# Sums of activations for the seven block products on VectorE instead of GpSimd, and other pairs of the down projection that take seven products

## The chip, the cores and the metric

The kernel runs on one core of one Trainium2 chip. The metric is the device time of one execution in microseconds (us); smaller is better. The kernel before took 1475.7 us, the median of three runs (1475.5 to 1476.75).

## The reference

One decoder layer for 256 tokens of width 2048, in float32: a normalised input is projected; a gated delta-rule branch and a block-sparse attention branch are mixed by gates and added to the residual; then a SwiGLU feed-forward follows. The change touches the last part alone:

```python
u = _rmsnorm(h, norm_ffn_w[l])
hid = jax.nn.silu(jnp.einsum('btd,df->btf', u, w_ffn_gate[l])) * jnp.einsum('btd,df->btf', u, w_ffn_up[l])
h = h + jnp.einsum('btf,fd->btd', hid, w_ffn_down[l])
```

The feed-forward width (`DFF`) is 5632, so `hid` has 44 slices (`kc`) of 128 features, and the down projection multiplies 256 x 5632 by 5632 x 2048.

## The kernel before, in words

**Split operands.** Every float32 operand is split into a rounded part (`hi`) and a rest (`lo`), and one product is three matmuls: hi·hi (L283), hi·lo (L284), lo·hi (L285). Weights are streamed from memory by SyncE in units of 128 x 1024 (L74, seven buffers). For each unit ScalarE casts the `hi` half (L87, tile `whi`) and VectorE subtracts it (L88, tile `wlo`); both have four buffers, and a unit is split three ahead of its use, so that the cast of a unit waits until TensorE is done with the unit four before it. The queues of ScalarE and VectorE are worked off in order: whatever stands ahead of a cast holds it back.

**Super jobs.** `super_job` works out two blocks of 512 columns for all 256 tokens at a time. Its weights come in pairs of units (`p`, 22 pairs in the down projection). A direct pair takes eight block products (24 matmuls). A pair marked as seven takes seven block products (21 matmuls), by Winograd's scheme: VectorE makes four half-unit sums of weights (L96, L97, L99, L100), four plan items instead of two are split (`b11`, half a unit, `b2`, and two called `t`), and four sums of activations are needed, for which `make_sums` has one call a pair. The feed-forward has eleven jobs with the pairs 3 and 5 as seven; the down projection has two jobs (`DOWN_USED`), the first with five seven pairs, the second with eight.

**`make_sums` (L962).** It adds hi and lo of two slices of activations (L967, 128 x 512, tile `f`), makes four 128 x 128 sums of the quarters (L970 to L973, tile `t`), casts them on ScalarE (L975, to `dsum` or `usum`) and subtracts the cast on VectorE (L976). `f` and `t` take the two buffers of `fsum` in turn, so the next pair's `t` waits for this pair's L975 and L976. Before the change L967 to L973 are on GpSimd. `down_sums` calls it for the eight pairs of `DOWN_PAIRS`; it is advanced by `tick()`, two ticks a pair of weights, after the five of the last feed-forward job's `swiglu`.

**After the last seven pair of a job** `after` copies four banks (L996) and GpSimd adds them up (L997 to L1000, and L1057 in the down projection).

The order of each engine's queue is set by a scheduler from the program, not by the order of the lines alone.

Of the kernel before, what the change touches and what calls it, by code (L numbers as in the profile page):

```python
# [17 lines left out]
T = 256  # L18
# [20 lines left out]

FFN_PAIRS = (3, 5)  # L40
FFN_ORDER = [[0, 1, 2, 4, 6, 3, 5, 7]] + [list(range(KM // 2))] * (DFF // 512 - 1)
DOWN_PAIRS = (4, 8, 12, 15, 18, 2, 6, 10)
DOWN_USED = [(4, 8, 12, 15, 18), DOWN_PAIRS]


def _super_jobs():

    jobs = [[(p, p in FFN_PAIRS) for p in order] for order in FFN_ORDER]
    return jobs + [[(p, p in used) for p in range(KF // 2)] for used in DOWN_USED]

# [62 lines left out]
def layer(ctx: ExitStack, tc: tile.TileContext, xT, xtok, params, consts, relt, w_bd, w, out):  # L113
    nc = tc.nc
# [193 lines left out]
    with tc.tile_pool(name="xin", bufs=4) as xin:  # L308
# [4 lines left out]
        for u in range(1, RAW):  # L313
            W.load(u)
            if u % 2:
                c = u // 2 + 1
# [632 lines left out]
    def hid(kc, n=1):  # L949
        t, k = (low, kc) if kc < H else (later["high"], kc - H)  # L950
        return t[:, k] if n == 1 else t[:, k:k + n]

    def fft(name, bufs):
        return later["ff"].tile([P, 512], F32, name=name, tag=name, bufs=bufs)
# [8 lines left out]
    def make_sums(g, c):  # L963

        c = c.bitcast(F32)
        f = fft("fsum", 2).rearrange("p (k t) -> p k t", k=2)
        nc.gpsimd.tensor_add(f, c[:, :, :T], c[:, :, T:])  # L967
        a11, a21, a12, a22 = f[:, 0, :P], f[:, 0, P:], f[:, 1, :P], f[:, 1, P:]
        t = fft("fsum", 2).rearrange("p (k t) -> p k t", k=4)
        nc.gpsimd.tensor_add(t[:, 0], a21, a22)  # L970
        nc.gpsimd.tensor_sub(t[:, 1], t[:, 0], a11)
        nc.gpsimd.tensor_sub(t[:, 2], a11, a21)
        nc.gpsimd.tensor_sub(t[:, 3], a12, t[:, 1])  # L973
        yield
        nc.scalar.copy(g[:, 0], t)  # L975
        nc.vector.tensor_sub(g[:, 1], t, g[:, 0].bitcast(F32))  # L976
        yield

# [2 lines left out]
    def ffn_setup():  # L981
        by_stage.close()
        later["ff"] = ff = ctx.enter_context(tc.tile_pool(name="ff", bufs=1))
        later["high"] = ff.tile([P, KF - H, 512], F32R, name="high")
        yield
        for p in FFN_PAIRS:
            usums[p] = ff.tile([P, 2, 4, P], F32R, name="usum", tag="sum", bufs=2)
            yield from make_sums(usums[p], uT[:, 2 * p:2 * p + 2])
# [41 lines left out]

    dsum = acts.tile([P, len(DOWN_PAIRS), 2, 4, P], F32R, name="dsum", tag="actA")

    def down_sums():
        for i, p in enumerate(DOWN_PAIRS):
            yield from make_sums(dsum[:, i], hid(2 * p, 2))
# [10 lines left out]
    chains.append(down_sums())  # L1046
    down = {p: lambda i=i: dsum[:, i] for i, p in enumerate(DOWN_PAIRS)}
    for j in range(2):
# [122 lines left out]
```

## Time and profile before

| | us |
|---|---|
| median of three runs | 1475.7 |
| the profiled execution | 1475.54 |
| its span, first to last instruction | 1473.8 |
| TensorE busy in the span | 1458.2 |
| VectorE busy | 1078.7 |
| ScalarE busy | 759.9 |
| GpSimd busy | 200.9 |

The profiled execution has 1.7 us around its span and lies 0.16 us under the median. Times in the rows below are us from the span's start. TensorE's matmuls are pipelined: each lasts about 0.39 us and a new one starts every 0.23 us, so a busy share near 1 says only that there was no gap. "Idle before" in brackets is the time in which the engine had nothing running before that row, with what ended it. The granted clock of TensorE is 1.00 at 2.4 GHz and 0.50 at 1.2 GHz.

### The profile page before, as it was taken

The page shows a single profiled execution, that of the slowest core. Times are in us where ns is not written, and L with a number is a line of the kernel's source. Part 1 is how long each engine was busy: PE and PEld are TensorE (multiplying, and loading weights), DVE is VectorE, ACT ScalarE, POOL GpSimd, SP SyncE. Part 2 cuts the span into 40 slices and gives each one's busy share as a digit, 9 for nine tenths or more (in the row PEclk, how much of TensorE's full clock was granted, in tenths as well). Part 3 has the DMA queues.
Part 4 walks back from the last instruction along what each step waited for, and adds up shares of the span by engine and source line. Part 5 has one row for each costly group of instructions (what it writes and reads, how often), then busy time and mean ns, then how long its engine had stood idle before and what let it go on. Part 6 is the DMA issues. An engine that isn't in the chain of part 4 may idle for free.

```text
span 1473.8 us, 19231 instructions
## 1 busy us (share of the span) xinstructions
PE 1458.2 (99%) x7077; PEld 1213.5 (82%) x7077; DVE 1078.7 (73%) x1452; ACT 759.9 (52%) x1100; POOL 200.9 (14%) x148
## 2 busy tenths in 40 slices
PE   9999999999999999999999999999999999899998
PEld 8888788888888888888888888888888887688887
DVE  6887679777664455555569888888888887777885
ACT  6664446635454444444545555555555554444553
POOL 0011000020000000000021223022222116405003
PEclk9999999999999999999999999999999999899999
DMA  9457545575456666668756666565665556557763
GB/s 375 147 197 183 162 136 176 163 170 186 143 159 180 195 195 186 189 191 258 217 173 200 214 191 193 170 203 187 214 207 192 190 184 198 163 197 224 231 204 109
DMA packets 78735, 282.05 MB, mean 191 GB/s; under 512 B 8880, under 2 KB 9520, under 8 KB 78256
## 3 DMA queue, kind: packets, MB, share of 16 engines
q1 hardware_dynamic: 76032, 272.30, 59.3%
q0 software_dynamic: 1472, 5.24, 1.1%
q10 hardware_dynamic: 1136, 3.28, 1.0%
q8 instruction: 55, 0.90, 0.2%
q14 instruction: 40, 0.33, 0.1%
HBM read 276.46 MB, written 4.33 MB: 191 GB/s over the span
## 4 chain that ended last, share of the span: by engine, by line
PE 93%; DVE 3%; ACT 1%; issue 1%; POOL 1%; DMA 0%; SPq 0%; DVEq 0%; POOLq 0%; ACTq 0%
PE ps L283 13%; PE ps L284 13%; PE ps L285 13%; PE ps L218 11%; PE ps L219 11%; PE ps L220 11%; PE ps L199 6%; PE ps L200 3%; PE pw L284 2%; PE pw L285 2%; PE pw L283 2%; PE pT L299 1%; DVE wlo L88 1%; ACT whi L87 1%; DVE dsum L976 0%
## 5 line engine op out<-in xcount | busy, mean ns | idle before, releaser
L88 DVE TENSOR_TENSOR wlo<-wraw,whi 128x1024 fp32r<-128x1024 f32 (+1 forms) x575 | 702.8, 1236 | 282.1 <-ACT whi L87 277.0
L87 ACT CAST whi<-wraw 128x1024 fp32r<-128x1024 f32 (+1 forms) x575 | 585.3, 1025 | 604.2 <-PE ps L285 233.6
L283 PE MATMUL ps<-whi,uT 128*128 128x512 f32 x572 | 223.8, 391 | 0.7 <-ACT whi L87 0.7
L285 PE MATMUL ps<-whi,uT 128*128 128x512 f32 x572 | 222.8, 390 | 0.0
L284 PE MATMUL ps<-wlo,uT 128*128 128x512 f32 x572 | 222.8, 389 | 0.0
L218 PE MATMUL ps<-whi,aT 128*128 128x512 f32 x512 | 204.5, 400 | 0.0
L219 PE MATMUL ps<-wlo,aT 128*128 128x512 f32 x512 | 200.1, 391 | 0.1
L220 PE MATMUL ps<-whi,aT 128*128 128x512 f32 x512 | 199.8, 390 | 0.0
L199 PE MATMUL ps<-aT,whi 128*128 128x512 f32 x384 | 139.0, 405 | 1.7 <-DVE aT L333 1.7
L283 PEld LDWEIGHTS ps<-whi,uT 128*128 128x128 f32 x572 | 107.4, 188 | 23.0 <-ACT whi L87 1.1
L285 PEld LDWEIGHTS ps<-whi,uT 128*128 128x128 f32 x572 | 107.4, 188 | 22.6
L284 PEld LDWEIGHTS ps<-wlo,uT 128*128 128x128 f32 x572 | 107.4, 188 | 21.9
L220 PEld LDWEIGHTS ps<-whi,aT 128*128 128x128 f32 x512 | 96.1, 188 | 20.3
L218 PEld LDWEIGHTS ps<-whi,aT 128*128 128x128 f32 x512 | 96.3, 188 | 18.8
L219 PEld LDWEIGHTS ps<-wlo,aT 128*128 128x128 f32 x512 | 96.3, 188 | 18.5 <-DVE wlo L88 0.4
L200 PE MATMUL ps<-aT,wlo 128*128 128x256 f32 x384 | 108.4, 282 | 0.9 <-DVE wlo L88 0.9
L199 PEld LDWEIGHTS ps<-aT,whi 128*128 128x128 f32 x384 | 73.5, 192 | 18.5 <-DVE aT L333 2.0
L284 PE MATMUL ps<-wlo,high 128*128 128x512 f32 x216 | 84.7, 392 | 0.4 <-DVE wlo L88 0.4
L283 PE MATMUL ps<-whi,high 128*128 128x512 f32 x216 | 84.6, 392 | 0.0
L285 PE MATMUL ps<-whi,high 128*128 128x512 f32 x216 | 84.6, 392 | 0.0
L997 POOL TENSOR_TENSOR ft<-ft 128x512 f32<-128x512 f32 x13 | 23.5, 1805 | 446.7 <-ACT ft L996 446.7
L200 PEld LDWEIGHTS ps<-aT,wlo 128*128 128x128 f32 x384 | 73.8, 192 | 1.3 <-DVE wlo L88 1.2
(395 smaller groups left out, 2004.3 us busy)
## 6 DMA issues: line engine op xcount, KB each, us to landing
wraw<-in_w SPq DMA_DIRECT2D x503, 512.0 KB, 4.2
xrow<-in_xtok SPq DMA_DIRECT2D x1, 2048.0 KB, 13.7
lb<-dm ACTq DMA_DIRECT2D x2, 1024.0 KB
xr<-in_xtok SPq DMA_DIRECT2D x8, 256.0 KB, 6.9
hsave<-h POOLq DMA_DIRECT2D x4, 512.0 KB, 5.5
hx<-hsave POOLq DMA_DIRECT2D x4, 512.0 KB, 7.8
xc<-in_xT SPq DMA_DIRECT2D x3, 512.0 KB, 7.5
bias<-in_relt SPq DMA_DIRECT2D x4, 256.0 KB, 4.0
```

The source lines that it names most:

```text
L87: self.last_hi = self.nc.scalar.copy(hi[:, f], raw[:, f])
L88: self.last_lo = self.nc.vector.tensor_sub(lo[:, f], raw[:, f], hi[:, f].bitcast(F32))
L199: nc.tensor.matmul(ps[:, j], hi[:, sl], act[:, kc], start=kc == 0, stop=False)
L200: nc.tensor.matmul(ps[:, j, :T], lo[:, sl], act[:, kc, :T], start=False, stop=kc == nk - 1)
L218: nc.tensor.matmul(ps[n], ah, hi[:, sl], start=kc == 0, stop=False)
L219: nc.tensor.matmul(ps[n], ah, lo[:, sl], start=False, stop=False)
L220: nc.tensor.matmul(ps[n], al, hi[:, sl], start=False, stop=kc == nk - 1)
L283: nc.tensor.matmul(ps, ah, hi[:, sl], start=i == use[0], stop=False)
L284: nc.tensor.matmul(ps, ah, lo[:, sl], start=False, stop=False)
L285: nc.tensor.matmul(ps, al, hi[:, sl], start=False, stop=i == use[-1])
L299: nc.tensor.transpose(p[n][:, i], srcs[n][:, i * P:(i + 1) * P], ident)
L997: nc.gpsimd.tensor_add(t[2], t[0], t[2])
```

## The change

```diff
-DOWN_PAIRS = (4, 8, 12, 15, 18, 2, 6, 10)
-DOWN_USED = [(4, 8, 12, 15, 18), DOWN_PAIRS]
+DOWN_PAIRS = (7, 9, 11, 13, 15, 17, 2, 5)
+DOWN_USED = [DOWN_PAIRS[:6], DOWN_PAIRS]
...
         f = fft("fsum", 2).rearrange("p (k t) -> p k t", k=2)
-        nc.gpsimd.tensor_add(f, c[:, :, :T], c[:, :, T:])
+        nc.vector.tensor_add(f, c[:, :, :T], c[:, :, T:])
         a11, a21, a12, a22 = f[:, 0, :P], f[:, 0, P:], f[:, 1, :P], f[:, 1, P:]
         t = fft("fsum", 2).rearrange("p (k t) -> p k t", k=4)
-        nc.gpsimd.tensor_add(t[:, 0], a21, a22)
-        nc.gpsimd.tensor_sub(t[:, 1], t[:, 0], a11)
-        nc.gpsimd.tensor_sub(t[:, 2], a11, a21)
-        nc.gpsimd.tensor_sub(t[:, 3], a12, t[:, 1])
-        yield
+        nc.vector.tensor_add(t[:, 0], a21, a22)
+        nc.vector.tensor_sub(t[:, 1], t[:, 0], a11)
+        nc.vector.tensor_sub(t[:, 2], a11, a21)
+        nc.vector.tensor_sub(t[:, 3], a12, t[:, 1])
         nc.scalar.copy(g[:, 0], t)
+        yield
         nc.vector.tensor_sub(g[:, 1], t, g[:, 0].bitcast(F32))
```

The five sums of a `make_sums` call go from GpSimd to VectorE, in all ten calls (two for the feed-forward, eight for the down projection). The first job of the down projection takes six seven pairs (7, 9, 11, 13, 15, 17) instead of five (4, 8, 12, 15, 18); the second takes eight as before, 2, 5, 7, 9, 11, 13, 15, 17 instead of 2, 4, 6, 8, 10, 12, 15, 18. The cast's line becomes L974. Neither SyncE's queue nor the number of weight units changes.

The first place is VectorE's queue at the start of the first down job (names: `wlo` the rest of a weight unit, `dsum` the split sums of the down projection, `fsum` the sums before the split, `high` the activations). Before:

```order
L976 TENSOR_TENSOR dsum_10440<-fsum_10583,dsum_10440 128x512
L88 TENSOR_TENSOR wlo_10534<-wraw_10471,whi_10533 128x1024
L976 TENSOR_TENSOR dsum_10440<-fsum_10632,dsum_10440 128x512
L88 TENSOR_TENSOR wlo_10566<-wraw_10491,whi_10565 128x1024
L976 TENSOR_TENSOR dsum_10440<-fsum_10686,dsum_10440 128x512
L88 TENSOR_TENSOR wlo_10591<-wraw_10511,whi_10590 128x512
```

With the change, from the same row on:

```order
L976 TENSOR_TENSOR dsum_10440<-fsum_10583,dsum_10440 128x512
L970 TENSOR_TENSOR fsum_10628<-fsum_10626 128x128
L972 TENSOR_TENSOR fsum_10628<-fsum_10626 128x128
L971 TENSOR_TENSOR fsum_10628<-fsum_10628,fsum_10626 128x128
L973 TENSOR_TENSOR fsum_10628<-fsum_10626,fsum_10628 128x128
L88 TENSOR_TENSOR wlo_10534<-wraw_10471,whi_10533 128x1024
L976 TENSOR_TENSOR dsum_10440<-fsum_10628,dsum_10440 128x512
L967 TENSOR_TENSOR fsum_10671<-high_6640 128x512
L970 TENSOR_TENSOR fsum_10673<-fsum_10671 128x128
L972 TENSOR_TENSOR fsum_10673<-fsum_10671 128x128
L88 TENSOR_TENSOR wlo_10566<-wraw_10491,whi_10565 128x1024
```

The sums now stand between the subtractions of weights in one queue, and the half unit (128x512) that opens a seven pair comes after eight whole ones from the first row, not after two.

The second place is ScalarE's queue in the same stretch (`whi` the rounded part of a weight unit). Before:

```order
L975 CAST dsum_10440<-fsum_10731 128x512
L87 CAST whi_10612<-wraw_10531 128x1024
L975 CAST dsum_10440<-fsum_10776 128x512
L87 CAST whi_10639<-wraw_10511 128x1024
L975 CAST dsum_10440<-fsum_10825 128x512
```

With the change, the casts of the same numbered sums (the fourth to the sixth):

```order
L974 CAST dsum_10440<-fsum_10718 128x512
L87 CAST whi_10636<-wraw_10563 128x1024
L87 CAST whi_10655<-wraw_10589 128x1024
L974 CAST dsum_10440<-fsum_10767 128x512
L87 CAST whi_10681<-wraw_10608 128x1024
L974 CAST dsum_10440<-fsum_10821 128x512
```

The casts of sums still stand ahead of casts of weights; the units between them are now those of direct pairs.

The third place is VectorE's queue in the fifth feed-forward job, at its second seven pair, where the sums of down pair 7 are begun:

```order
 L88 TENSOR_TENSOR wlo_8181<-wraw_8115,whi_8180 128x512
+L967 TENSOR_TENSOR fsum_10581<-high_6640 128x512
 L96 TENSOR_TENSOR wraw_8115<-wraw_8115 128x512
 L88 TENSOR_TENSOR wlo_8201<-wraw_8135,whi_8200 128x1024
 L97 TENSOR_TENSOR wraw_8115<-wraw_8135,wraw_8115 128x512
+L970 TENSOR_TENSOR fsum_10583<-fsum_10581 128x128
 L99 TENSOR_TENSOR wraw_8135<-wraw_8135,wraw_8115 128x512
+L971 TENSOR_TENSOR fsum_10583<-fsum_10583,fsum_10581 128x128
 L100 TENSOR_TENSOR wraw_8135<-wraw_8135 128x512
 L88 TENSOR_TENSOR wlo_8221<-wraw_8115,whi_8220 128x1024
+L972 TENSOR_TENSOR fsum_10583<-fsum_10581 128x128
+L973 TENSOR_TENSOR fsum_10583<-fsum_10581,fsum_10583 128x128
```

Five more instructions stand there between those that make the last two plan items of a seven pair.

## Rows read from the trace of the kernel before

**Rows 1.** The page, part 1: busy time, share of the span, instructions.
```profile
span 1473.8 us, 19231 instructions
PE 1458.2 (99%) x7077; PEld 1213.5 (82%) x7077; DVE 1078.7 (73%) x1452; ACT 759.9 (52%) x1100; POOL 200.9 (14%) x148
```

**Rows 2.** Windows: length, PE, PEld, DVE, ACT, POOL busy, clock, DMA share, GB/s.
```profile
1235.00:1250.00 15.00, 15.00 (x72) 12.47 (x71) 9.17 (x12) 6.31 (x9) 11.76 (x15) 1.00 0.37 120
1250.00:1256.00 6.00, 2.77 (x10) 1.42 (x8) 4.01 (x5) 1.57 (x2) 5.02 (x6) 0.97 0.00 0
1256.00:1266.00 10.00, 7.28 (x16) 4.98 (x17) 6.53 (x6) 3.92 (x5) 8.91 (x10) 0.50 0.44 127
```

**Rows 3.** Timeline of TensorE, first down job: start, length, engine, line, operation [idle before].
```profile
1227.08 0.39 PE L283 MATMUL ps<-whi,low 128*128 128x512 f32 x1
...
1240.45 0.39 PE L285 MATMUL ps<-whi,low 128*128 128x512 f32 x1
...
1249.76 0.39 PE L283 MATMUL pw<-whi,high 128*128 128x512 f32 x1
...
1250.44 0.39 PE L283 MATMUL ps<-whi,dsum 128*128 128x512 f32 x1
1252.05 0.50 PE L284 MATMUL ps<-wlo,dsum 128*128 128x512 f32 x1 [1.21 <-DVE wlo L88]
...
1258.07 0.80 PE L284 MATMUL pw<-wlo,dsum 128*128 128x512 f32 x1 [2.65 <-DVE wlo L88]
...
1266.18 0.40 PE L285 MATMUL ps<-whi,high 128*128 128x512 f32 x1
```

**Rows 4.** Timeline of ScalarE in the same stretch.
```profile
1253.29 0.62 ACT L975 CAST dsum<-fsum 128x512 fp32r<-128x512 f32 x1 [3.62 <-POOL fsum L973]
1253.82 1.04 ACT L87 CAST whi<-wraw 128x1024 fp32r<-128x1024 f32 x1
1258.89 0.62 ACT L975 CAST dsum<-fsum 128x512 fp32r<-128x512 f32 x1 [4.03 <-POOL fsum L973]
```

**Rows 5.** Timeline of GpSimd in the same stretch: one call's four sums.
```profile
1255.30 0.77 POOL L970 TENSOR_TENSOR fsum<-fsum 128x128 f32<-128x128 f32 x1 [0.69 <-DVE dsum L976]
...
1256.89 1.43 POOL L971 TENSOR_TENSOR fsum<-fsum 128x128 f32<-128x128 f32 x1
1258.40 0.45 POOL L973 TENSOR_TENSOR fsum<-fsum 128x128 f32<-128x128 f32 x1
```

**Rows 6.** Groups by line: busy us, mean ns of one, idle us before.
```profile
L96 DVE TENSOR_TENSOR wraw<-wraw 128x512 f32<-128x512 f32 x35 | 24.3, 696 | 1.2
...
L606 DVE TENSOR_TENSOR prod<-lb,X 128x128 f32<-128x128 f32 x2 | 0.8, 394 | 0.1
L568 DVE TENSOR_TENSOR mc<-mc,cst 128x128 f32<-128x128 f32 x2 | 0.6, 280 | 0.0
```

**Rows 7.** Timeline of VectorE at the start of the first down job.
```profile
1233.85 1.23 DVE L88 TENSOR_TENSOR wlo<-wraw,whi 128x1024 fp32r<-128x1024 f32 x1
1234.99 0.69 DVE L976 TENSOR_TENSOR dsum<-fsum,dsum 128x512 fp32r<-128x512 f32 x1
```

**Rows 8.** Timelines of VectorE and TensorE, first feed-forward job.
```profile
766.17 1.23 DVE L976 TENSOR_TENSOR usum<-fsum,usum 128x512 fp32r<-128x512 f32 x1 [3.50 <-ACT usum L975]
...
787.62 0.50 PE L283 MATMUL ps<-whi,uT 128*128 128x512 f32 x1 [0.71 <-ACT whi L87]
```

**Rows 9.** Timelines of VectorE and TensorE, fifth feed-forward job, end of its second seven pair.
```profile
953.80 2.36 DVE L88 TENSOR_TENSOR wlo<-wraw,whi 128x1024 fp32r<-128x1024 f32 x2 [1.07 <-ACT whi L87]
...
956.10 0.39 PE L284 MATMUL pw<-wlo,usum 128*128 128x512 f32 x1
```

**Rows 10.** Windows, as in rows 2: part of the second down job.
```profile
1400.00:1425.00 25.00, 25.00 (x112) 20.72 (x111) 21.61 (x24) 14.23 (x15) 0.00 (x0) 1.00 0.71 219
```

**Rows 11.** Timelines of VectorE and TensorE near the end of the second down job.
```profile
1459.50 1.73 DVE L88 TENSOR_TENSOR wlo<-wraw,whi 128x1024 fp32r<-128x1024 f32 x1 [0.51 <-ACT whi L87]
...
1461.28 0.50 PE L284 MATMUL ps<-wlo,high 128*128 128x512 f32 x1 [0.42 <-DVE wlo L88]
```

More of the change, by code (lines that the diff above doesn't have):

```diff
@@ L966, in make_sums @@
         f = fft("fsum", 2).rearrange("p (k t) -> p k t", k=2)
-        nc.gpsimd.tensor_add(f, c[:, :, :T], c[:, :, T:])
+        nc.vector.tensor_add(f, c[:, :, :T], c[:, :, T:])
         a11, a21, a12, a22 = f[:, 0, :P], f[:, 0, P:], f[:, 1, :P], f[:, 1, P:]
         t = fft("fsum", 2).rearrange("p (k t) -> p k t", k=4)
-        nc.gpsimd.tensor_add(t[:, 0], a21, a22)
-        nc.gpsimd.tensor_sub(t[:, 1], t[:, 0], a11)
-        nc.gpsimd.tensor_sub(t[:, 2], a11, a21)
-        nc.gpsimd.tensor_sub(t[:, 3], a12, t[:, 1])
+        nc.vector.tensor_add(t[:, 0], a21, a22)
+        nc.vector.tensor_sub(t[:, 1], t[:, 0], a11)
+        nc.vector.tensor_sub(t[:, 2], a11, a21)
+        nc.vector.tensor_sub(t[:, 3], a12, t[:, 1])
+        nc.scalar.copy(g[:, 0], t)
         yield
-        nc.scalar.copy(g[:, 0], t)
         nc.vector.tensor_sub(g[:, 1], t, g[:, 0].bitcast(F32))
```

## The prediction, made before the changed kernel was run

> **What bounds the kernel now.** I read the page first, then windows over the feed-forward and the down projection, then the timelines of single engines where a window showed a gap. The page says that TensorE is busy 99% of the span [rows 1], so time can come only from fewer matmuls or from the few gaps. The windows show one gap that matters: from 1235 to 1250 us TensorE has none; from 1250 to 1256 it is busy 2.77 of 6.00 us, and from 1256 to 1266 its granted clock is 0.50, which is 1.2 instead of 2.4 GHz [rows 2]. In the same stretch GpSimd is busy 13.9 of 16 us, and for the first six microseconds the DMA share is 0.00: the weights are there, or their buffers are not yet free.
>
> The size of that loss: undisturbed, sixty matmuls start between 1227.08 and 1240.45 us, a spacing of 13.37 / 59 = 0.2266 us. From 1250.44 to 1266.18 us I counted 23 steps from one start to the next in 15.74 us [rows 3]; undisturbed they take 5.21 us. **10.53 us** are lost, to the waits for `wlo` and `whi` and to the slow clock after them.
>
> The cause is a chain through three engines. The cast of the sums on ScalarE (L975) sat 3.62 and 4.03 us waiting for GpSimd's last sum, and the cast of the weights behind it in the queue could only start after it [rows 4]. GpSimd could start a call's quarter sums only when VectorE had finished the last call's subtraction, and took from 1255.30 to 1258.85 us for four of them; one took 0.45 us, another 1.43 [rows 5]. So the casts came in step with the calls, 5.6 us apart (1253.29 to 1258.89), while TensorE eats a direct unit in 12 x 0.2266 = 2.72 us. The lead of the splits was used up just when pair 4, the first with seven products, came.
>
> **The change, part by part.** *One product fewer.* Six seven pairs instead of five in the first job take away three matmuls: 3 x 0.2266 = 0.68 us, as TensorE is the bound. In exchange VectorE gets four half-unit sums and one and a half subtractions more, and ScalarE one and a half casts; they are in the cycle counted below.
>
> *The sums on VectorE.* One call becomes 128 x 512 once, like L96 at 0.70 us, and 128 x 128 four times. The nearest rows for the latter are L568 at 0.28 us (plain operands, as here) and L606 at 0.39 (one strided operand) [rows 6]. I take 0.28 and keep 0.39 as upper end. A call is 0.70 + 4 x 0.28 = 1.8 us, in the queue that needs its result, and no wait for another engine remains but the cast. The first row says against GpSimd's 3.5 us for the quarter sums alone that the chain gets shorter. The Trainium skill, Perfetto Trace Analysis, section "Optimizing Scalar/DVE Operations", speaks against such a move: the two engines share a read port of SBUF, "so offloading operations between those two might not help". By it the loss stays, and only the 0.68 us go; that case is priced among the rivals. The rows bear the sharing out in part (the same sum takes 0.45 or 1.43 us), but with the sums moved GpSimd has nothing to read in this stretch.
>
> *Does VectorE keep up in the first job?* This is the step on which the sum hangs. The row at 1234.99 us stands at the same place in both orders [rows 7]. From it to the end of the first full-unit subtraction after L100 of pair 7 (the first `t` item), the new order has 59 instructions: 10 subtractions of whole units at 1.23 us, 1 of half a unit, 4 sums of weights, 2 evictions L960 and 6 times L967 at 0.70 each (9.1), 8 times L976 at 0.69 (5.5), 28 quarter sums at 0.28 (7.8). That makes 12.3 + 9.1 + 5.5 + 7.8 = 34.7 us, ready at 1269.7. It is too much, since an instruction that doesn't need the one before it starts 0.09 us before that ends (1233.85 + 1.23 against 1234.99 [rows 7]); for some 39 of the 59 this is 3.5 us, ready at 1266.2. TensorE wants this item 82 matmuls after 1249.76 us (three direct pairs, 9 matmuls, one more), at 1268.3. So the gap there is between 0 and 1.4 us. I take **0.3**, since the spacing of rows is what the queue shows and the casts of sums add small waits. At 0.39 us a quarter sum it would be 1.4 + 28 x 0.114 = 4.6: the upper end. What stands behind the sums in both queues, the splits of units 6 to 15, is late by less than its lead of about three units until then.
>
> *After that* a seven pair and a direct one in turn take 45 x 0.2266 = 10.2 us of TensorE and, on VectorE, five whole units and five half-size rows, 5 x 1.23 + 5 x 0.70 less 10 x 0.09 = 8.8 us; ScalarE has five and a half casts at 1.04 us a whole one, 5.7 us. No gap: the second job already runs this alternation, and a window of it shows TensorE busy 25.00 of 25.00 us with VectorE at 21.61 [rows 10]. The price without this cover is a rival.
>
> *The two feed-forward calls* put 2 x 1.8 us on VectorE and take them off GpSimd, where VectorE sat idle 3.50 us for them; the gap of 0.71 us on TensorE 16 us later [rows 8] comes from two seven pairs in a row, which stay. Nought.
>
> *The first down call*, begun in the fifth feed-forward job, puts 1.8 us on VectorE ahead of the last item of a seven pair. That item started after 1.07 us of idleness, was ready at 953.80 + 1.23 = 955.03 and wanted at 956.10 [rows 9]: room for 2.1 us. Nought, 0.2 at the upper end.
>
> *The end.* GpSimd's additions after the last seven pair move one direct pair, 5.4 us, away from the end. A subtraction of 1.73 us there makes TensorE wait 0.42 us [rows 11]; the additions last long enough to stay beside it. Nought, a gain of 0.4 at best. The DMA issues of SP and GpSimd keep their order; loads wait on VectorE's subtractions, some seven units ahead of use, so they are no term.
>
> **Sum**, against the profiled execution's own 1475.54 us: 1475.54 - 10.53 - 0.68 + 0.3 = 1464.6. That execution lies 0.16 us under the median of the runs, so I forecast **1464.8 us**.
>
> **The rivals.** *Gap and slow clock at pair 7.* If the quarter sums cost nearer to 0.39 us, TensorE waits 2 to 4.6 us, and the clock may fall, as it did after the waits of 1.21 to 2.65 us [rows 2, 3]. Some 5 us at half clock cost 2.5 more: 1464.3 + 2.3 + 2.5 = 1469 in the middle, 1466 to 1472. For it speaks the thin margin; against it that L568 has the operands of this case.
>
> *The small gaps go too.* With none at pair 7 and those of 0.71 and 0.42 us gone: 1463.2.
>
> *The change doesn't do what it says.* VectorE's reads cost what GpSimd's did, the casts of sums still come 5.6 us apart, and the same 10.5 us are lost at pairs 4 to 6 on whole units: 1475.54 - 0.68 = 1474.9. This is what the quoted section amounts to. Against it: with GpSimd idle, VectorE's 128 x 512 rows take 0.70 us.
>
> *VectorE becomes the bound, and it is slower.* Place: the alternation of seven and direct pairs. It decides where VectorE's cycle passes 10.2 us, which is at 1.52 us a whole unit; next to GpSimd's additions one takes 1.73 [rows 11]. Then a cycle is 11.3 us, 1.05 over, and fourteen seven pairs give 1464.3 + 14.7 = 1479.0. Against it: GpSimd is idle in nearly all of these cycles, and the window of the second job shows no gap [rows 10].
>
> **How the numbers follow.** Forecast (1463.8 to 1466) 0.72; small gaps gone 0.08; gap with slow clock 0.12; loss stays 0.05; VectorE bound 0.03. The range 1463.0 to 1469.0 holds the first two and half of the third, 0.86. A measurement of this kernel tells about 0.2% (3 us) from no change: faster has the first three cases, 0.92; same 0.05; slower 0.03.
>
> **What would show it.** Right: no slow clock anywhere between 1235 and 1290 us, no TensorE wait there over 1.4 us, quarter sums at 0.28 us or less on VectorE, ScalarE no longer waiting on GpSimd for `dsum`, three matmuls fewer. Wrong: a wait on `wlo` at pair 7 with the clock at 0.50 behind it (second case), or TensorE still short of units before it (third).

## The result, and the profile after

| | before | after |
|---|---|---|
| median of the timed runs, us | 1476.14 (1475.5 to 1476.75, 4 runs) | 1463.93 (1461.33 to 1466.7, 4 runs) |
| the profiled execution, us | 1475.54 | 1466.7 |
| its span, us | 1473.8 | 1464.9 |

Both kernels were timed on the same chip. The time ratio is 0.9918, 95% interval 0.9898 to 0.9937: the changed kernel is faster by 0.8%, which is more than the 0.2% that can be told from no change. Forecast were 1464.8 us, between 1463.0 and 1469.0.

The page of the changed kernel, part 1, answers to [rows 1]:

```profile
span 1464.9 us, 19230 instructions
...
PE 1453.0 (99%) x7074; PEld 1209.8 (83%) x7074; DVE 1090.3 (74%) x1508; ACT 763.3 (52%) x1102; POOL 159.3 (11%) x98
```

Three matmuls are gone from TensorE (7077 to 7074) and fifty instructions from GpSimd (148 to 98: ten calls of five sums). VectorE has fifty-six more: the fifty, four sums of weights and two subtractions of weights.

The same three windows as in [rows 2] (length, PE, PEld, DVE, ACT, POOL busy, clock, DMA share, GB/s):

```profile
1235.00:1250.00 15.00, 15.00 (x72) 12.52 (x71) 14.75 (x28) 8.01 (x11) 0.00 (x0) 1.00 0.62 179
1250.00:1256.00 6.00, 6.00 (x28) 4.96 (x27) 5.86 (x13) 3.53 (x4) 0.00 (x0) 1.00 0.66 182
1256.00:1266.00 10.00, 10.00 (x46) 8.27 (x45) 9.89 (x21) 4.72 (x7) 0.00 (x0) 1.00 0.47 154
```

The gap, the clock of 0.50 (1.2 GHz) and the six microseconds without a transfer are gone. TensorE starts 74 matmuls in the sixteen microseconds after 1250 where it started 26. GpSimd does nothing there, and VectorE, busy 19.71 of these 31 us before [rows 2], now is for 30.50: it is close to the limit, and hardly waits.

ScalarE in that stretch (start, length, engine, line, operation, in brackets the idle time before and what ended it):

```profile
1249.33 0.62 ACT L974 CAST dsum<-fsum 128x512 fp32r<-128x512 f32 x1 [1.54 <-DVE fsum L973]
1249.86 1.05 ACT L87 CAST whi<-wraw 128x1024 fp32r<-128x1024 f32 x1
1252.17 1.05 ACT L87 CAST whi<-wraw 128x1024 fp32r<-128x1024 f32 x1 [1.27 <-issue]
1253.13 0.61 ACT L974 CAST dsum<-fsum 128x512 fp32r<-128x512 f32 x1
1254.89 1.05 ACT L87 CAST whi<-wraw 128x1024 fp32r<-128x1024 f32 x1 [1.15 <-issue]
1256.43 0.62 ACT L974 CAST dsum<-fsum 128x512 fp32r<-128x512 f32 x1 [0.48 <-DVE fsum L973]
```

Against [rows 4], the casts of sums come 3.3 to 3.8 us apart (1249.33, 1253.13, 1256.43) instead of 5.6, and the idle time ahead of one is 1.54 us at most, not 4.03. A cast of weights behind it is no longer too late.

VectorE's groups by line between 1220 and 1290 us, shapes apart (busy us, mean ns of one, idle us before), answer to [rows 5, 6]:

```profile
L967 DVE TENSOR_TENSOR fsum<-high 128x512 f32<-128x512 f32 x5 | 3.5, 691 | 0.1
L970 DVE TENSOR_TENSOR fsum<-fsum 128x128 f32<-128x128 f32 x7 | 2.0, 291 | 0.2
L972 DVE TENSOR_TENSOR fsum<-fsum 128x128 f32<-128x128 f32 x7 | 2.0, 285 | 0.0
L976 DVE TENSOR_TENSOR dsum<-fsum,dsum 128x512 fp32r<-128x512 f32 x8 | 5.5, 686 | 0.0
```

A quarter sum takes 0.285 to 0.291 us on VectorE, against 0.45 to 1.43 on GpSimd. The row to look at twice is L976, which the change did not touch. In the same view of the kernel before (1220 to 1290 us) it was:

```profile
L976 DVE TENSOR_TENSOR dsum<-fsum,dsum 128x512 fp32r<-128x512 f32 x8 | 8.8, 1096 | 12.3 <-ACT dsum L975 12.3
```

It fell from 1.10 to 0.69 us, and its idle time from 12.3 us to nothing. Why is shown by the last experiment.

**How the stage is measured below.** The start of the down projection wanders from execution to execution (see the end), so whole times differ by more than some experiments are worth. The stage itself repeats to some hundredths: from the first matmul that reads `low` to the end of the last matmul of the kernel. Before, these two are [rows 3] at 1227.08 and this row:

```profile
1469.62 0.39 PE L285 MATMUL ps<-whi,high 128*128 128x512 f32 x1
```

That is 1469.62 + 0.39 - 1227.08 = 242.93 us. Of the changed kernel:

```profile
1229.27 0.39 PE L283 MATMUL ps<-whi,low 128*128 128x512 f32 x1
...
1460.77 0.39 PE L285 MATMUL ps<-whi,high 128*128 128x512 f32 x1
```

1461.16 - 1229.27 = 231.89 us, 11.04 less. The tail from there to the end of the span (the last addition and its store) is 3.8 us before and 3.7 after. "Stage" in the expectations includes the tail (246.7 and 235.6 us).

### The profile page after: what moved, and what is told of

It is laid out like the page before. It is cut to its first block, busy times and chain, and to the rows that moved or that the text cites. A ratio compares the mean times of both kernels' runs of the same rounds, so it can differ in the third digit from the quotient of the medians.

```text
span 1464.9 us, 19230 instructions
## 1 busy us (share of the span) xinstructions
PE 1453.0 (99%) x7074; PEld 1209.8 (83%) x7074; DVE 1090.3 (74%) x1508; ACT 763.3 (52%) x1102; POOL 159.3 (11%) x98
## 4 chain that ended last, share of the span: by engine, by line
PE 92%; DVE 3%; DMA 2%; issue 1%; ACT 1%; POOL 0%; SPq 0%; DVEq 0%; ACTq 0%
PE ps L284 13%; PE ps L285 13%; PE ps L283 13%; PE ps L218 11%; PE ps L219 11%; PE ps L220 10%; PE ps L199 5%; PE ps L200 3%; PE pw L284 2%; PE pw L285 2%; PE pw L283 2%; DMA lb<-dm 1%; DVE wlo L88 1%; PE pT L299 1%; DVE cacc L465 1%
## 5 line engine op out<-in xcount | busy, mean ns | idle before, releaser
L88 DVE TENSOR_TENSOR wlo<-wraw,whi 128x1024 fp32r<-128x1024 f32 (+1 forms) x577 | 702.7, 1232 | 276.8 <-ACT whi L87 273.8
L285 PE MATMUL ps<-whi,high 128*128 128x512 f32 x210 | 81.7, 389 | 0.0
L283 PE MATMUL ps<-whi,high 128*128 128x512 f32 x210 | 81.5, 389 | 0.0
```

What stands on the lines that cost most here:

```text
L88: self.last_lo = self.nc.vector.tensor_sub(lo[:, f], raw[:, f], hi[:, f].bitcast(F32))
L283: nc.tensor.matmul(ps, ah, hi[:, sl], start=i == use[0], stop=False)
L285: nc.tensor.matmul(ps, al, hi[:, sl], start=False, stop=i == use[-1])
```

## The experiments

All the times, worked out in that way from each run's profiled execution; ratios are against the kernel before on the same chip:

| | median us | ratio (95%) | low to last matmul | tail |
|---|---|---|---|---|
| before | 1473.9 to 1476.1 | 1 | 242.93 | 3.8 |
| changed | 1463.93 | 0.9918 (0.9898 to 0.9937) | 231.89 | 3.7 |
| 1 sums on VectorE, old pairs | 1464.17 | 0.992 (0.9905 to 0.9935) | 232.28 | 3.7 |
| 2 sums on GpSimd, new pairs | 1471.9 | 0.9976 (0.9965 to 0.9986) | 239.62 | 3.8 |
| 3 quarter sums twice | 1464.55 | 0.9929 (0.9911 to 0.9948) | 233.96 | 3.8 |
| 4 five pairs in the first job | 1463.21 | 0.9914 (0.9899 to 0.9929) | 232.60 | 3.8 |
| 5 seven, the last 19 | 1462.59 | 0.9925 (0.9912 to 0.9937) | 230.77 | 4.8 |
| 6 feed-forward sums on GpSimd | 1463.47 | 0.9928 (0.9912 to 0.9943) | 231.93 | 3.7 |
| 7 cast behind the yield | 1463.09 | 0.9926 (0.9913 to 0.994) | 231.89 | 3.7 |
| 8 every second pair from 4 | 1463.21 | 0.9926 (0.9912 to 0.9939) | 232.26 | 3.8 |
| 9 seven from 5 | 1463.45 | 0.992 (0.9905 to 0.9935) | 231.71 | 3.8 |
| 10 seven from 6 to 18 | 1462.24 | 0.9914 (0.9899 to 0.9929) | 230.97 | 3.7 |
| 11 eight in both jobs | 1462.67 | 0.9917 (0.9902 to 0.9931) | 231.32 | 3.7 |
| 12 quarter sums alone on VectorE | 1469.64 | 0.9962 (0.995 to 0.9975) | 237.94 | 3.8 |

### 1 and 2: each half of the change alone

```diff
 # 1: the changed kernel
-DOWN_PAIRS = (7, 9, 11, 13, 15, 17, 2, 5)
-DOWN_USED = [DOWN_PAIRS[:6], DOWN_PAIRS]
+DOWN_PAIRS = (4, 8, 12, 15, 18, 2, 6, 10)
+DOWN_USED = [(4, 8, 12, 15, 18), DOWN_PAIRS]
```

> The first half of the change alone: the sums on VectorE, the pairs of the kernel before (five seven pairs in the first job, pair 4 first). Theory (the loss came from casts of weights held behind casts of sums that waited for GpSimd): the gap at pair 4 goes nearly whole, since VectorE's rows up to the first t item of pair 4 add up to some 15.4 us from the first L976, which makes it ready 1.6 us before TensorE wants it. Down stage (first matmul of the down projection to the end of the span) 235.6 + 0.7 = 236 to 238 us against 246.7 before; device time about 1465. Rival (the later pairs do most of it, and VectorE's sums pile up in front of an early pair 4): a gap of 3 us or more with the granted clock at 0.50 behind it, down stage 240 to 245 us, device time 1469 to 1474.

Measured: 232.28 us, 10.65 less than before, with TensorE waiting 0.42 us in all, at the end of the second job as before. The move of the sums alone takes the whole loss away, and pair 4, which comes 16 us sooner than pair 7, finds its units ready.

```diff
 # 2: the kernel before
-DOWN_PAIRS = (4, 8, 12, 15, 18, 2, 6, 10)
-DOWN_USED = [(4, 8, 12, 15, 18), DOWN_PAIRS]
+DOWN_PAIRS = (7, 9, 11, 13, 15, 17, 2, 5)
+DOWN_USED = [DOWN_PAIRS[:6], DOWN_PAIRS]
```

> The second half alone: the new pairs (7 first, six in the first job), the sums still on GpSimd. Theory: the casts of weights still come one between two casts of sums, 4.7 to 5.7 us apart, against 2.72 us a direct unit on TensorE; a lead of three units is gone after three or four of them, so TensorE waits at direct units before pair 7, 2 to 3 us a unit, 6 to 10 us in all with the clock, down stage 241 to 246 us, device time 1470 to 1475. Rival (a seven pair that comes late enough is all that is needed): no wait, down stage 235.6 us, device time 1464.

Measured: 239.62 us, 3.31 less than before; the stage is 243.4 us, inside the forecast. TensorE's waits in the down stage by what it waited for (us in total, times, longest):

```profile
PE ps L284 <- DVE wlo L88: 3.8, 5, 1.0
PE ps L283 <- ACT whi L87: 1.4, 3, 0.5
PE pw L284 <- DVE wlo L88: 0.7, 1, 0.7
```

The sums of GpSimd still hold the casts back, and TensorE waits 5.9 us, 0.7 of it at the end of the second job. The other 5.2 us are eight waits of at most 1.0 us between 1255 and 1276 us, where before four waits of up to 2.65 us came within 11 us (two of them in [rows 3]). Seven of the eight stand at direct units ahead of pair 7, as forecast, but they are shorter than the 2 to 3 us a unit that I had given. The clock stays at 1.00, as the window over them shows (columns as above):

```profile
1250.00:1280.00 30.00, 24.73 (x100) 18.09 (x99) 20.00 (x21) 13.31 (x16) 14.27 (x19) 1.00 0.40 119
```

The later pairs thus mend 0.68 us by the matmuls and 2.6 us of the rest. The two halves overlap: 10.65 + 3.31 is 13.96, together they bring 11.04.

### 3: VectorE's new work doubled

```diff
         nc.vector.tensor_add(t[:, 0], a21, a22)
+        nc.vector.tensor_add(t[:, 0], a21, a22)
         nc.vector.tensor_sub(t[:, 1], t[:, 0], a11)
+        nc.vector.tensor_sub(t[:, 1], t[:, 0], a11)
...
```

Likewise the other two: each of the four is made twice.

> The changed kernel with each of the four 128 x 128 sums of make_sums written twice, 28 more such rows on VectorE ahead of the first t item of pair 7 (0.20 to 0.29 us each, 5.6 to 8 us). Theory (VectorE has about 1.6 us to spare there and no more): the gap at pair 7 opens, 4 to 6.5 us of waits on wlo, and the granted clock falls to 0.50 behind it if a single wait is near 2.65 us; down stage 239.6 to 246 us, device time 1468 to 1474. Rival (the sums lie beside other work in any case): no wait, down stage unchanged at 235.6 us.

Measured: 233.96 us, 2.07 more than the changed kernel; the theory had 4.0 to 10.4 more, and its place was wrong too. At pair 7 there is no wait. VectorE's rows in this run (lines below the sums are four higher here; L967 of `low` opens the seventh call, the one for pair 2), and the matmul that takes the last of them:

```profile
1261.53 0.68 DVE L967 TENSOR_TENSOR fsum<-low 128x512 f32<-128x512 f32 x1
1262.13 0.68 DVE L100 TENSOR_TENSOR wraw<-wraw 128x512 f32<-128x512 f32 x1
1262.74 1.22 DVE L88 TENSOR_TENSOR wlo<-wraw,whi 128x1024 fp32r<-128x1024 f32 x1
...
1264.83 0.39 PE L284 MATMUL pw<-wlo,dsum 128*128 128x512 f32 x1
```

Pair 7's first `t` item is ready at 1262.74 + 1.22 = 1263.96, and the matmul that takes it starts at 1264.83: 0.87 us to spare, where the changed kernel has 1.56. The seventh call now begins only here, among the sums of weights; in the changed kernel it stands ahead of pair 7's first subtraction. The scheduler put the later calls behind the weights that are due sooner. The bill comes at 1276 to 1289 us instead, as two waits of 0.8 and 0.2 us and late starts around them, 2.0 us in all. So VectorE's slack is real but small, and the order gives way before TensorE does.

### 4: five seven pairs instead of six

```diff
-DOWN_USED = [DOWN_PAIRS[:6], DOWN_PAIRS]
+DOWN_USED = [DOWN_PAIRS[:5], DOWN_PAIRS]
```

> The changed kernel with five seven pairs (7, 9, 11, 13, 15) in the first down job instead of six. Theory (TensorE is the bound there): three matmuls more, 0.68 us, down stage 236.3 us, no wait anywhere in the first job; device time 1464.6, which the timing can't tell from 1463.9. Rival (VectorE is the bound in the alternation of seven and direct pairs): the stage gets shorter, not longer, by the work of one seven pair that VectorE no longer has, 1 us or more.

Measured: 232.60 us, 0.71 more than with six. A seven pair is worth its three matmuls (0.68) and nothing else.

### 5, 9, 10 and 11: more seven pairs

```diff
-DOWN_PAIRS = (7, 9, 11, 13, 15, 17, 2, 5)
-DOWN_USED = [DOWN_PAIRS[:6], DOWN_PAIRS]
+DOWN_PAIRS = (7, 9, 11, 13, 15, 17, 19, 5)
+DOWN_USED = [DOWN_PAIRS[:7], DOWN_PAIRS]
```

> Edit: the changed kernel with a seventh pair of seven products (19) in the first down job. Theory (TensorE is the only bound once the sums are on VectorE, and the alternation of seven and direct pairs leaves VectorE 8.8 of 10.2 us): three matmuls fewer are 0.68 us, so the down stage (first matmul on low to the end of the span) lasts 234.9 us where the changed kernel has 235.6, with no TensorE wait over 0.8 us in it. Rival (VectorE has no room for another seven pair beside the sums of the last calls): new waits for wlo behind pair 15, stage at 235.6 or more.

Measured: 230.77 us to the last matmul, even 0.44 better than 231.89 - 0.68, with no wait listed on TensorE, but the tail grew by 1.0 us, so the stage is 235.5. The end of this kernel, on GpSimd and on TensorE:

```profile
1453.10 3.76 POOL L1057 TENSOR_TENSOR ft<-ft,hx 128x512 f32<-128x512 f32 x3
...
1455.35 0.39 PE L285 MATMUL ps<-whi,high 128*128 128x512 f32 x1
```

With pair 19 as the last seven pair of the second job, too, GpSimd's additions end at 1456.86, after the last matmul (1455.74). The edit was meant for the first job; by the list that both jobs share it moved the end.

```diff
 # 9                                         # 10: (6, 8, 10, 12, 14, 16, 18, 4)
-DOWN_PAIRS = (7, 9, 11, 13, 15, 17, 2, 5)
-DOWN_USED = [DOWN_PAIRS[:6], DOWN_PAIRS]
+DOWN_PAIRS = (5, 7, 9, 11, 13, 15, 17, 2)
+DOWN_USED = [DOWN_PAIRS[:7], DOWN_PAIRS]
```

> Edit: the changed kernel with the down pairs 5, 7, 9, 11, 13, 15, 17 in the first job, and 2 beside them in the second. Theory (a pair costs its three matmuls as long as the last seven pair of the second job stays 17, which leaves GpSimd's last additions time to end beside TensorE): from the first matmul on low to the end of the last matmul 231.89 - 0.68 = 231.2 us, the tail behind it 3.7 us as in the changed kernel, the stage 234.9 to 235.0 us. Rival (a call of sums every second pair from 5 on is too much for VectorE): waits of 0.8 us or more between 1260 and 1300 us, stage 235.7 us or more.

> Edit: the changed kernel with the down pairs 6, 8, 10, 12, 14, 16, 18 in the first job, and 4 beside them in the second. Theory: three matmuls fewer, and the gap at the end of the second job, which costs 1.08 us with 17 as the last pair, costs 0.8 with 18 as in the run with the old pairs: 231.89 - 0.68 - 0.28 = 230.9 us from the first matmul on low to the end of the last, tail 3.7 us, stage 234.6 us. Rival (GpSimd's additions now end behind TensorE, as with 19): tail 4 to 4.8 us, stage 235.0 to 235.7 us.

Measured: 231.71 us for number 9, half a microsecond short of the theory. No wait is listed between 1260 and 1300 us, since one shorter than a matmul leaves no idle time; the starts on TensorE show it:

```profile
1278.59 0.39 PE L283 MATMUL pw<-whi,dsum 128*128 128x512 f32 x1
1279.09 0.50 PE L284 MATMUL pw<-wlo,dsum 128*128 128x512 f32 x1
1279.43 0.40 PE L285 MATMUL pw<-whi,dsum 128*128 128x512 f32 x1
```

Steps of 0.50 and 0.34 us instead of 0.23 lose 0.38, most of the half microsecond, while VectorE is busy 19.96 of 20.00 us around them: the rival in kind, at half its size. Number 10: 230.97 us against 230.9 expected, tail 3.7, stage 234.7 against 234.6. TensorE's only wait in its down stage:

```profile
PE ps L284 <- DVE wlo L88: 0.4, 1, 0.4
```

This is the best version found: its stage is 0.9 us shorter than the changed kernel's, 0.92 to the last matmul with the same tail. The medians (1462.24, 1461.19 to 1463.75, and 1463.93) can't show so little; the stage can.

```diff
 # 11
+DOWN_PAIRS = (4, 6, 8, 10, 12, 14, 16, 18)
+DOWN_USED = [DOWN_PAIRS[:8], DOWN_PAIRS]
```

> Edit: the changed kernel with the down pairs 4, 6, 8, 10, 12, 14, 16, 18 in both jobs. Theory: six matmuls fewer than the changed kernel are 1.36 us; the wait of the run with every second pair from 4 comes again once or twice (0.8 us each): 230.4 to 231.8 us from the first matmul on low to the end of the last, stage 234.1 to 235.5 us. Rival (VectorE falls further behind with two pairs more): waits of 2 us or more up to 1310 us, half clock behind them, stage over 237 us.

Measured: 231.32 us, inside the range, with one wait of 0.38 us near 1281 us, beside that at the end, and VectorE busy 20.00 of 20 us around it. It saves three matmuls more than number 10 and is 0.35 us slower: here VectorE's room ends.

### 6 and 7: parts that should be worth nothing

```diff
 # 6: make_sums has eng=nc.vector for its five sums, and
-            yield from make_sums(usums[p], uT[:, 2 * p:2 * p + 2])
+            yield from make_sums(usums[p], uT[:, 2 * p:2 * p + 2], nc.gpsimd)
 # 7
-        nc.scalar.copy(g[:, 0], t)
         yield
+        nc.scalar.copy(g[:, 0], t)
```

> Edit: the changed kernel with the sums of the two feed-forward calls back on GpSimd, those of the eight down calls on VectorE. Theory (the two calls are worth nothing either way): the feed-forward from its first matmul on uT to the first on low lasts 476.0 to 476.2 us as in both kernels, the down stage 235.6 us. Rival (some of the gain came from the feed-forward calls): the feed-forward is over 0.5 us longer, or the gap of 0.71 us near 786 us grows.

> Edit: the changed kernel with the cast of the sums behind the yield again, as before the change. Theory (the place of the yield decides nothing, since the scheduler orders the queues by what each instruction needs): the same order on every engine, down stage 235.6 us; the total differs from the changed kernel's only by when the down projection starts, 1224 to 1229 us. Rival (the earlier cast is what lets the next call begin sooner): casts of the sums wait on ScalarE, TensorE waits over 0.5 us at pair 7, stage 236.5 us or more.

Measured: from the first matmul on `uT` to the last of the kernel, number 6 takes 708.02 us and the changed kernel 708.01. The feed-forward calls are worth nothing. Number 7 changes no engine's order, so it is the changed kernel once more: 231.89 us again, to the hundredth, while its span is 1461.3 and not 1464.9 us.

### 8: a call of sums every two pairs, as early as the ticks allow

```diff
-DOWN_PAIRS = (7, 9, 11, 13, 15, 17, 2, 5)
+DOWN_PAIRS = (4, 6, 8, 10, 12, 14, 2, 16)
```

> Edit: the changed kernel with the down pairs 4, 6, 8, 10, 12, 14 in the first job (and 2, 16 in the second), so that each call of sums has only two pairs of weights of time. Theory (VectorE's own rows set the limit): a cycle of one seven and one direct pair takes 8.8 us of VectorE for the weights and 1.8 + 0.6 us for a call, 11.2 against TensorE's 10.2; pair 4 still comes in time, and some 1 us a cycle is lost after it: waits on wlo of 1 to 4 us in all between 1260 and 1300 us, VectorE busy without a pause there, down stage 236.6 to 239.6 us. Rival (the calls can be put off far enough): no wait, stage 235.6 us. Rival (half clock follows as in the kernel before): over 240 us.

Measured: 232.26 us. Windows of this kernel (columns as above):

```profile
1250.00:1265.00 15.00, 15.00 (x68) 12.43 (x67) 14.96 (x22) 10.03 (x12) 0.00 (x0) 1.00 0.64 200
1265.00:1285.00 20.00, 19.59 (x85) 15.48 (x85) 20.00 (x34) 11.53 (x14) 0.00 (x0) 1.00 0.55 174
1285.00:1310.00 25.00, 25.00 (x112) 20.54 (x111) 23.48 (x26) 15.80 (x19) 3.40 (x2) 1.00 0.72 249
```

VectorE has no pause from 1265 to 1285 us, as the theory said, but the price is one listed wait of 0.41 us, for a cast on ScalarE, and some late starts behind it, 1.0 us in all between 1281 and 1285: the lowest of the 1 to 4 that I had given. No slow clock follows. The wait of 0.7 us at the end of the second job is not in this run, so the stage, 236.0, lies between theory (236.6) and first rival (235.6). The cycle count of 11.2 us against 10.2 left out that the units are split some three ahead: four cycles over by 1.0 us would be mostly paid from that lead, though no run here isolates it.

### 12: the first sum of a call back on GpSimd

```diff
 # the changed kernel with the old pairs, as in 1, and
-        nc.vector.tensor_add(f, c[:, :, :T], c[:, :, T:])
+        nc.gpsimd.tensor_add(f, c[:, :, :T], c[:, :, T:])
```

> Edit: the changed kernel with the pairs of before and the first sum of each call (128 x 512) back on GpSimd; the quarter sums and the place of the cast stay. Theory (what held the casts back was the chain subtraction, quarter sums, cast, subtraction; the first sum can be made while the cast and the subtraction run): no wait at pair 4, from the first matmul on low to the end of the last 232.3 us and stage 236.0 us as with all sums on VectorE. Rival (any step on GpSimd in the chain costs its hand-over and slows VectorE's rows beside it): TensorE waits 1 to 5 us around 1250 to 1260 us, stage 237 to 242 us.

Measured: 237.94 us, 5.66 more than number 1, which differs in this one line. My theory fell: the first sum is off the chain that I had drawn, and yet half of the loss is back. The stage of 241.7 us lies in the rival's range. TensorE's waits in the down stage:

```profile
PE pw L284 <- DVE wlo L88: 2.8, 2, 1.8
PE ps L284 <- DVE wlo L88: 0.7, 2, 0.4
```

and behind the longest, from 1257 us on, seven matmuls start 0.43 us apart instead of 0.23, half clock again, which leaves the window's granted clock at 0.89:

```profile
1250.00:1265.00 15.00, 12.15 (x45) 9.19 (x45) 12.98 (x20) 7.76 (x9) 4.65 (x2) 0.89 0.63 207
```

The reason stands in the timelines. First GpSimd:

```profile
1235.50 2.20 POOL L967 TENSOR_TENSOR fsum<-high 128x512 f32<-128x512 f32 x1 [11.00 <-DVE fsum L973]
...
1250.82 3.35 POOL L967 TENSOR_TENSOR fsum<-low 128x512 f32<-128x512 f32 x1 [3.44 <-DVE fsum L973]
1260.93 1.29 POOL L967 TENSOR_TENSOR fsum<-high 128x512 f32<-128x512 f32 x1 [6.75 <-DVE fsum L973]
```

then VectorE, and the matmul behind it:

```profile
1235.34 1.22 DVE L88 TENSOR_TENSOR wlo<-wraw,whi 128x1024 fp32r<-128x1024 f32 x1
1236.48 1.78 DVE L976 TENSOR_TENSOR dsum<-fsum,dsum 128x512 fp32r<-128x512 f32 x1
...
1251.20 1.22 DVE L88 TENSOR_TENSOR wlo<-wraw,whi 128x1024 fp32r<-128x1024 f32 x1
1252.33 0.68 DVE L976 TENSOR_TENSOR dsum<-fsum,dsum 128x512 fp32r<-128x512 f32 x1
1254.21 0.29 DVE L970 TENSOR_TENSOR fsum<-fsum 128x128 f32<-128x128 f32 x1 [1.20 <-POOL fsum L967]
...
1255.90 0.50 PE L284 MATMUL pw<-wlo,dsum 128*128 128x512 f32 x1 [1.77 <-DVE wlo L88]
```

L967 takes 1.29 us on GpSimd when it starts in a pause of VectorE (the last row of the three). Issued at 1250.82, amid rows of VectorE one right behind the other, it takes 3.35: it ends at 1254.17, and 1254.17 - 1.29 = 1252.88 is within 0.13 us of the end of VectorE's unbroken run (1252.33 + 0.68 = 1253.01). By these times it did its work only when VectorE paused. The other way round, L976 takes 1.78 us instead of 0.68 when it meets a running L967: it ends 0.56 us after GpSimd does (1238.26 and 1237.70). In these rows the two engines take turns, a whole instruction at a time; work of one is waiting time of the other. Which of them goes first varies: in the row of 1235.50 GpSimd got in right behind the L88 that was running, and in the next two calls, too, it got in ahead of L976, which took 1.79 and 1.62 us; at 1250.82 two more rows of VectorE passed ahead of it. What decides this the runs do not show.

VectorE so lost 3.15 us on these three L976, and then waited 1.20 us for the late L967. The subtraction of weights behind that wait sets TensorE's longest, which ends at 1255.90. The wait is not the price of a hand-over between engines: with 1.29 us of work L967 would have ended at 1252.11, before VectorE was through with L976 (an estimate from the rows above).

The Trainium skill, SBUF — State Buffer, section "🔬 SBUF: two separate sides", says this of a VectorE operation with two inputs in SBUF beside a GpSimd operation that reads SBUF: whichever starts first has the shared ports for its whole instruction, and the other is blocked. These rows agree with it, and add that VectorE's rows, one right behind the other, once kept GpSimd out for a whole run of them.

That the two engines met in the kernel before, too, is seen in L976, 1.10 us there and 0.69 with GpSimd idle. One such meeting in the kernel before, VectorE's row and then GpSimd's:

```profile
1259.54 1.23 DVE L976 TENSOR_TENSOR dsum<-fsum,dsum 128x512 fp32r<-128x512 f32 x1 [1.53 <-ACT dsum L975]
...
1258.93 1.28 POOL L967 TENSOR_TENSOR fsum<-high 128x512 f32<-128x512 f32 x1
```

Here, too, L976 ends 0.56 us after L967 (1260.77 and 1260.21).

## Why the prediction was right

**The loss.** 10.53 us were to go; the move of the sums alone (number 1) took 10.65 from the first matmul on `low` to the last. Right in size and place.

**Why it goes.** I said that the chain of subtraction, quarter sums, cast and subtraction gets shorter, and called the sharing of the two engines borne out "in part". Number 12 shows that this weighed the two wrongly. With the chain short, and only one sum a call beside it on GpSimd, 5.66 us come back. Shown is that a short chain alone is not enough; how the 10.65 us divide between chain and sharing is not, since no run slowed the chain with GpSimd idle. An estimate from rows: the four quarter sums from 1255.30 to 1258.85 us took 3.55 where four at 0.45 take 1.8 [rows 5], and the L976 behind them 1.23 where it takes 0.69; so some 2 of the 5.6 us between two casts were sharing.

**The sentence against the change.** By the Trainium skill, Perfetto Trace Analysis, section "Optimizing Scalar/DVE Operations", moving work between the two might not help, and I gave the case in which the loss stays 0.05. Its premise, the sharing, holds here more strongly than I thought. What it warns of did not come: the move ended the sharing instead of shifting it, and a quarter sum that cost GpSimd 0.45 us or more now costs VectorE 0.29.

**VectorE's walk to pair 7.** The forecast was ready between 1266.2 and 1269.7, wanted at 1268.3, gap 0 to 1.4, taken 0.3. The changed kernel (VectorE's first `t` item, and the matmul that takes it):

```profile
1267.73 1.22 DVE L88 TENSOR_TENSOR wlo<-wraw,whi 128x1024 fp32r<-128x1024 f32 x1
```

```profile
1270.51 0.39 PE L284 MATMUL pw<-wlo,dsum 128*128 128x512 f32 x1
```

The stage starts 1229.27 - 1227.08 = 2.19 us later in this execution. Taken off, the item is ready at 1267.73 + 1.22 - 2.19 = 1266.76 and wanted at 1268.32. The wanted time was right to 0.02 us; the ready time lies near the early end, 1.6 us ahead. The early end was the one that counts the overlap of 0.09 us from row to row, and it was the better guide: quarter sums that don't need the one before start 0.20 to 0.21 us apart, not 0.29. So no gap, where I took 0.3 from between the ends, and no slow clock.

**One product fewer** was to be 0.68 us and is 0.71 (number 4). **The alternation** was to leave VectorE room: number 10 adds a seventh pair to the first job at its full price, so yes; numbers 8, 9 and 11 show how soon the room ends once the calls of sums fall into it. **The feed-forward calls** were nought and are (number 6); its gap of 0.71 us [rows 8] stands unchanged.

**The end** was the one step with the wrong sign. I said nought, a gain of 0.4 at best, since GpSimd's additions move away from the end. They met a subtraction of weights all the same. VectorE and GpSimd, then TensorE:

```profile
1450.41 2.01 DVE L88 TENSOR_TENSOR wlo<-wraw,whi 128x1024 fp32r<-128x1024 f32 x1 [1.47 <-ACT whi L87]
...
1450.05 4.77 POOL L1057 TENSOR_TENSOR ft<-ft,hx 128x512 f32<-128x512 f32 x3
```

```profile
1452.48 0.50 PE L284 MATMUL ps<-wlo,high 128*128 128x512 f32 x1 [0.69 <-DVE wlo L88]
```

The subtraction takes 2.01 us there, not 1.73, and TensorE waits 0.69 us, not 0.42 [rows 11]: 0.28 us lost.

**The sum** by its own terms, as measured: -10.65 - 0.71 + 0 + 0.28 = -11.08, against 11.04 seen in the stage and 10.91 predicted. That the two agree to 0.13 us is partly luck: the 0.3 us forecast at pair 7 did not come, and the 0.28 us at the end, which were not forecast, made up for them. The span fell by 8.9 us only, because in this execution the down projection began 2.19 us later; the median over four runs, which begin at different times, fell by 12.2. So a median 0.9 us from the forecast says little by itself; the four runs of the changed kernel lie 5.4 us apart. The stage is what bears the sum out.

## What to carry to other kernels

When two engines share a way into memory, moving work from the one to the other is not a zero-sum trade: ask how long the same rows take with the other engine idle and busy, for the rows of both, and count the stretched ones as the price of leaving the work where it is. A cast of small sums that stands in a queue ahead of casts of weights should wait for nothing slow, since everything behind it waits too. And where TensorE is the bound, measure a change over its own stage, from a matmul that both kernels have to the last one; the whole time carries the drift of all stages ahead.

## What the runs showed that I had not expected

The sharing of number 12, in its strictness: 1.29 us became 3.35 on GpSimd, and 0.68 became 1.78 on VectorE.

The same early instructions don't take the same time. The first matmul on `low` started between 1223.59 us (number 3) and 1229.27 (changed) in executions whose order up to the feed-forward is the same but for the sums. The distance from the first matmul on `uT` to it is 476.0 to 476.4 us in all of them, so the drift arises before 750 us. The changed kernel's profiled execution had the latest start of all, and clock and busy time in its first 20 us are lower than in the kernel before. The windows of the changed kernel, and then of the kernel before:

```profile
0.00:20.00 20.00, 16.07 (x76) 14.17 (x77) 12.97 (x23) 14.99 (x27) 0.20 (x4) 0.91 0.90 343
```

```profile
0.00:20.00 20.00, 17.20 (x76) 15.18 (x77) 14.06 (x25) 15.29 (x27) 0.55 (x5) 1.00 0.92 345
```

These 20 us are not the whole of it: number 12 is busy 15.80 us in them, at the same 0.91, and has its first matmul on `uT` at 749.76 us, the changed kernel at 753.15. What makes the start wander I did not test.

Half clock did not follow every wait: eight waits of at most 1.0 us within 21 us left it at 1.00 (number 2), waits of 1.08 and 1.77 us within 5 us were followed by 0.43 us a matmul (number 12).
